# Seven products of quarters for eight in the down projections of a two-layer decoder trunk

## The chip, the cores and the metric

One core of one Trainium2 chip runs the whole program in one launch. The metric is the device time of one execution in microseconds (us). The kernel before takes 990.58 us, the median of three runs (990.31 to 990.7).

## What is computed

A two-layer trunk on x of 256 positions by 1024 features, all in float32. Cut to what matters here:

```
def swiglu(h, w_gate, w_up, w_down):
    return (silu(h @ w_gate) * (h @ w_up)) @ w_down      # 1024 -> 2816 -> 1024

for layer in (0, 1):
    h = h + 0.5 * swiglu(rmsnorm(h), ffn1_w_gate, ffn1_w_up, ffn1_w_down)
    h = h + mixer(rmsnorm(h))      # layer 0: dilated windows, layer 1: blocks
    h = h + 0.5 * swiglu(rmsnorm(h), ffn2_w_gate, ffn2_w_up, ffn2_w_down)
return rmsnorm(h)
```

So there are four SwiGLU stages, named f10 and f20 (layer 0) and f11 and f21 (layer 1), and each ends in a product of activations 256 x 2816 with down weights 2816 x 1024. These four products are the subject.

## The kernel before, in words

**Every float32 product is three products.** `parts_of` (L84) and `pieces_of` (L143) split an operand into a rounded high part, written by ScalarE (ACT) as a copy (L154 for weights), and the rest, written by VectorE (DVE) as a subtraction (L155). `product` (L180) then issues high by high (L183), high by low (L185) and low by high (L187), all into one PSUM accumulator. The tiles of weights are called wh and wl. Each name has its pool of 8 buffers, and a buffer holds 128 x 1024; raw weights have 4 buffers of 1 MB, filled by SyncE's (SP) DMA queue.

**A SwiGLU stage** is `ffn_blocks` and then `down`. `ffn_blocks` goes over 22 blocks f of 128 hidden features, two at a time: gate and up products (L194 128x512, L197 128x256, weights stationary), then ACT and DVE join, scale and multiply them (L391 to L410), and `parts_of` leaves block f as the tile act_f, features on partitions and the 256 positions side by side, high and low.

**The down product** (L359) takes its weights in 11 units u of two blocks of rows, k = 2u and 2u+1, each row block 128 x 1024. Outputs are four accumulators of 128 positions by 512 columns, (t, c) with t the half of the positions and c the half of the columns; in the program's words they are dn_f_d with t, c and an offset. For the first 18 blocks k, PE goes through all four outputs for each k: 12 matmuls of 128x512, which is 24 for a unit. The weights of the last four k are held, and each output in turn gets its last 12 matmuls, is added to h by DVE (L385, a scalar_tensor_tensor with the norm's factor), and `done` starts the next norm on it. In f10, f20 and f11 the turn is (0,0), (1,0), (0,1), (1,1), the list TURNED. In f21, the last stage, output (1,1) is two accumulators of 256 columns all the way, so that the last piece before the end is small.

**PSUM** has five banks in the pool accp (accumulators) and three in trp (transposes, and the norm's small products). `down` uses four of accp in three stages and five in f21.

**The order** on each engine is set by the framework's scheduler out of the program order, buffers and dependences; each engine runs its own queue in order. Tiles of the pool xp (one buffer for each name) hold the normed input x of a stage, one tile for each k; ap holds 22 tiles of activations; pp holds softmax tiles in the attention stages.

Of the kernel before, what the change touches and what calls it, by code (L numbers as in the profile page):

```python
# [62 lines left out]
def trunk(ctx: ExitStack, tc: tile.TileContext, a: dict, out: bass.AP):  # L63
# [291 lines left out]


    TURNED = [(0, 0, 0, 512), (1, 0, 0, 512), (0, 1, 0, 512), (1, 1, 0, 512)]

    def down(name, w, blocks, scale, segs, done, tail=4):  # L359


        accs = [acc(f"dn_{name}_{t}_{c}_{o}")[:, :n] for t, c, o, n in segs]
# [18 lines left out]
        for i, (t, c, o, n) in enumerate(segs):
            for k, ws in held:
                product(accs[i:i + 1], *lhs(k, t), [cols(i, ws)], False, k == KF - 1)
            hc = h[:, t, c * 512 + o:c * 512 + o + n]
            nc.vector.scalar_tensor_tensor(hc, accs[i], scale[t], hc, op0=ALU.mult, op1=ALU.add)  # L385
            done(*segs[i])
# [377 lines left out]
```

## Time and profile before

| | |
|---|---|
| median of three runs | 990.58 us (990.31 to 990.7) |
| the profiled execution | 990.6 us, of which its span is 988.8 us |
| PE busy in the span | 977.8 us, 99% |
| DVE busy | 692.7 us, 70% |
| ACT busy | 590.8 us, 60% |
| granted TensorE clock, mean | 0.999 |
| weights read by SP's queue | 175.55 MB, 54.9% of the 16 engines' span |

How to read it: the profile is of one execution. Its span runs from the first instruction to the last on the core, and the device time is 1.8 us longer. "Busy" counts a matmul from its start to its modelled end, and matmuls overlap, so that the mean of one (378 ns) is longer than the distance to the next; the distances between starts say what a matmul costs. "Idle before" is time in which the engine had nothing to run just before an instruction, with what ended it. A stage's limit is read from the windows and from the waits inside that stage.

### The profile page before, as it was taken

The page shows a single profiled execution, that of the slowest core. Times are in us where ns is not written, and L with a number is a line of the kernel's source. Part 1 is how long each engine was busy: PE and PEld are TensorE (multiplying, and loading weights), DVE is VectorE, ACT ScalarE, POOL GpSimd, SP SyncE. Part 2 cuts the span into 40 slices and gives each one's busy share as a digit, 9 for nine tenths or more (in the row PEclk, how much of TensorE's full clock was granted, in tenths as well). Part 3 has the DMA queues.
Part 4 walks back from the last instruction along what each step waited for, and adds up shares of the span by engine and source line. Part 5 has one row for each costly group of instructions (what it writes and reads, how often), then busy time and mean ns, then how long its engine had stood idle before and what let it go on. Part 6 is the DMA issues. An engine that isn't in the chain of part 4 may idle for free.

```text
span 988.8 us, 14084 instructions
## 1 busy us (share of the span) xinstructions
PE 977.8 (99%) x5297; PEld 832.1 (84%) x5297; DVE 692.7 (70%) x1248; ACT 590.8 (60%) x1068; POOL 58.9 (6%) x72
## 2 busy tenths in 40 slices
PE   9999999999999999999999999999999999999997
PEld 6888888888888888888888888888877888888886
DVE  7977764577786777774488777646677868777642
ACT  6766553567776656653476566436677756655531
POOL 3000000022400000000000000000142000000000
PEclk9999999999999999999999999999999999999999
DMA  9985565464344566665555665655534346555611
GB/s 319 288 261 172 175 234 188 138 206 168 128 129 132 166 194 195 207 204 181 169 171 178 206 200 183 213 192 172 190 129 149 124 148 186 182 174 199 224 43 42
DMA packets 127236, 177.00 MB, mean 179 GB/s; under 512 B 3520, under 2 KB 106176, under 8 KB 127168
## 3 DMA queue, kind: packets, MB, share of 16 engines
q1 hardware_dynamic: 126736, 175.55, 54.9%
q8 instruction: 41, 0.67, 0.3%
q10 hardware_dynamic: 432, 0.55, 0.2%
q14 instruction: 27, 0.22, 0.1%
HBM read 175.04 MB, written 1.05 MB: 178 GB/s over the span
## 4 chain that ended last, share of the span: by engine, by line
PE 93%; ACT 3%; DVE 2%; DMA 1%; issue 0%; SPq 0%; POOLq 0%; POOL 0%; ACTq 0%; DVEq 0%
PE f_g L194 16%; PE f_u L194 16%; PE f_u L197 8%; PE f_g L197 8%; PE dn_f_d L183 8%; PE dn_f_d L185 8%; PE dn_f_d L187 8%; PE qk_a L183 1%; PE qk_a L187 1%; PE qk_a L185 1%; PE x_n L275 1%; DVE wl_ao L348 1%; PE kv_b L183 1%; PE ot_ao L183 1%; PE q_b L183 1%; PE ot_ao L187 1%
## 5 line engine op out<-in xcount | busy, mean ns | idle before, releaser
L194 PE MATMUL f_g<-x_n,wh_f_g 128*128 128x512 f32 x688 | 180.2, 393 | 0.0
L194 PE MATMUL f_u<-x_n,wh_f_u 128*128 128x512 f32 x688 | 178.0, 390 | 0.0
L155 DVE TENSOR_TENSOR wl_f_d<-raw_f_d,wh_f_d 128x1024 fp32r<-128x1024 f32 x88 | 107.1, 1224 | 85.9 <-ACT wh_f_d L154 75.0
L194 PEld LDWEIGHTS f_u<-x_n,wh_f_u 128*128 128x128 f32 x688 | 129.0, 188 | 26.7
L194 PEld LDWEIGHTS f_g<-x_n,wh_f_g 128*128 128x128 f32 x688 | 123.9, 189 | 23.0 <-DVE x_n L92 0.4
L154 ACT ACTIVATE wh_f_d<-raw_f_d 128x1024 fp32r<-128x1024 f32 x88 | 91.4, 1056 | 85.3 <-PE dn_f_d L187 84.8
L155 DVE TENSOR_TENSOR wl_f_g<-raw_f_g,wh_f_g 128x1024 fp32r<-128x1024 f32 x86 | 102.7, 1221 | 43.9 <-PE f_g L197 31.6
L183 PE MATMUL dn_f_d<-wh_f_d,act_f 128*128 128x512 f32 (+1 forms) x374 | 115.3, 378 | 0.0
L185 PE MATMUL dn_f_d<-wl_f_d,act_f 128*128 128x512 f32 (+1 forms) x374 | 115.2, 378 | 0.0
L187 PE MATMUL dn_f_d<-wh_f_d,act_f 128*128 128x512 f32 (+1 forms) x374 | 114.9, 378 | 0.0
L155 DVE TENSOR_TENSOR wl_f_u<-raw_f_u,wh_f_u 128x1024 fp32r<-128x1024 f32 x86 | 104.8, 1220 | 8.1 <-ACT wh_f_u L154 8.0
L197 PE MATMUL f_u<-x_n,wl_f_u 128*128 128x256 f32 x688 | 103.2, 283 | 0.0
L197 PE MATMUL f_g<-x_n,wl_f_g 128*128 128x256 f32 x688 | 103.1, 283 | 0.0
L197 PEld LDWEIGHTS f_g<-x_n,wl_f_g 128*128 128x128 f32 x688 | 96.3, 190 | 6.6
L154 ACT ACTIVATE wh_f_g<-raw_f_g 128x1024 fp32r<-128x1024 f32 x86 | 90.3, 1054 | 12.8 <-PE f_g L194 4.0
L197 PEld LDWEIGHTS f_u<-x_n,wl_f_u 128*128 128x128 f32 x688 | 91.7, 192 | 0.1
L154 ACT ACTIVATE wh_f_u<-raw_f_u 128x1024 fp32r<-128x1024 f32 x86 | 87.4, 1050 | 7.2 <-PE dn_f_d L187 3.3
L187 PEld LDWEIGHTS dn_f_d<-wh_f_d,act_f 128*128 128x128 f32 x374 | 69.0, 188 | 13.1
L185 PEld LDWEIGHTS dn_f_d<-wl_f_d,act_f 128*128 128x128 f32 x374 | 69.0, 188 | 13.0
L183 PEld LDWEIGHTS dn_f_d<-wh_f_d,act_f 128*128 128x128 f32 x374 | 68.8, 188 | 13.0 <-DVE j_f_g L392 0.6
L408 ACT ACTIVATE j_f_g<-j_f_g 128x256 f32<-128x256 f32 x88 | 36.0, 416 | 59.3 <-DVE j_f_g L407 57.8
L90 DVE TENSOR_TENSOR act_f<-j_f_g,act_f 128x256 fp32r<-128x256 f32 x88 | 37.0, 423 | 33.7 <-ACT act_f L94 33.7
(208 smaller groups left out, 1446.2 us busy)
## 6 DMA issues: line engine op xcount, KB each, us to landing
raw_f_d<-in_ffn_w_down_dram SPq DMA_DIRECT2D x44, 1024.0 KB, 4.9
raw_f_g<-in_ffn_w_gate_dram SPq DMA_DIRECT2D x43, 1024.0 KB, 5.3
raw_f_u<-in_ffn_w_up_dram SPq DMA_DIRECT2D x43, 1024.0 KB, 5.3
raw_qka<-in_a_w_qkv_dram SPq DMA_DIRECT2D x16, 512.0 KB, 4.2
raw_va<-in_a_w_qkv_dram SPq DMA_DIRECT2D x4, 1024.0 KB, 5.1
raw_ao<-in_a_w_o_dram SPq DMA_DIRECT2D x4, 1024.0 KB, 4.9
raw_kvb<-in_kv_w_dram SPq DMA_DIRECT2D x8, 512.0 KB, 4.0
raw_qb<-in_b_w_q_dram SPq DMA_DIRECT2D x4, 1024.0 KB, 5.0
```

The source lines that it names most:

```text
L90: nc.vector.tensor_sub(lo, src, hi.bitcast(F32))
L154: nc.scalar.activation(wh, r, AF.Copy)
L155: nc.vector.tensor_sub(wl, r, wh.bitcast(F32))
L183: nc.tensor.matmul(ac, xh, wh, start=first, stop=False)
L185: nc.tensor.matmul(ac, xh, wl, start=False, stop=False)
L187: nc.tensor.matmul(ac, xl, wh, start=False, stop=last)
L194: nc.tensor.matmul(ac, wh, flat(x), start=first and i == 0, stop=False)
L197: nc.tensor.matmul(ac[:, :S], wl, x[:, 0, :], start=False, stop=last and i == len(ws) - 1)
L275: nc.tensor.transpose(tr[:, (2 * i + t) * P:(2 * i + t + 1) * P], h[:, t, k * P:(k + 1) * P], ident)
L348: self.rest.append(lambda wl=wl, raw=raw, wh=wh: nc.vector.tensor_sub(wl, raw, wh.bitcast(F32)))
L408: nc.scalar.activation(g, g, AF.Silu)
```

## The change

In each down product four of the eleven units, u in SEVEN = (1, 3, 5, 7), are multiplied by Winograd's form of Strassen's scheme. Such a unit is a 2 x 2 product of quarters: activations a11, a21 (block k = 2u, the halves of the positions), a12, a22 (block 2u+1), weights b11, b12 (block 2u, the halves of the columns), b21, b22 (block 2u+1). Eight products of quarters (24 matmuls of 128x512) become seven (21), of four sums of activations and four sums of weights.

- `add_up` (in `ffn_blocks`) forms the four sums s1 to s4 of a unit's activations when its second block is done: four DVE operations of 128x128, then `parts_of` of 128x512 (one ACT, one DVE).
- `sevenths` forms the sums of the weights, t1 with t3 in one DVE subtraction of 128x1024, t2 and t4 in one of 128x512 each, and splits b11 (128x512) and b21 with b22, t1 with t3, t2 with t4 (128x1024 each): four wh and four wl buffers for a unit where it was two of each. Its temporaries take the xp tiles x0 to x3; for that `gain` now lays two k of x into one tile.
- Three products of a unit add straight into the outputs (0,0), (0,1), (1,0) with the other units; p1, p5 and p7 gather in the three banks of trp and p6 in the fifth of accp over the four units.
- After u = 7 `gather` adds p1, p5, p6 and p7 to h: one ACT copy and two DVE additions (u, v), and six scalar_tensor_tensor, all 128x512.
- In f21 output (1,1) is one accumulator of 512 columns up to k = 17, closed after u = 8; only the held four k go into two halves of 256, in trp banks.

The diff's core:

```
+SEVEN = (1, 3, 5, 7)
...
+    def sevenths(name, j, raw):
+        both = [xp.tile([P, 2, 512], F32, tag=f"x{2 * (j % 2) + i}", name=f"t_{name}_{i}") for i in range(2)]
+        (t1, t3), (t2, t4) = [(b[:, 0], b[:, 1]) for b in both]
+        nc.vector.tensor_sub(both[0], raw[:, :, 512:], raw[:, 0, :].rearrange("p (c n) -> p c n", n=512))
+        (b11,), one = split(f"{name}_a", raw[:, 0, :512], 512)
+        one()
+        (b21, b22), two = split(f"{name}_b", raw[:, 1, :], 1024)
+        two()
+        nc.vector.tensor_sub(t2, raw[:, 1, 512:], t1)
+        nc.vector.tensor_sub(t4, raw[:, 1, :512], t2)
+        (w1, w3), three = split(f"{name}_c", flat(both[0]), 1024)
+        three()
+        (w2, w4), four = split(f"{name}_d", flat(both[1]), 1024)
+        four()
+        return b11, b21, b22, w1, w3, w2, w4
...
+        def gather():
+            close(0, 0, p1)
+            u, v = [atile([P, 512], name=f"u_{name}_{i}") for i in range(2)]
+            nc.scalar.activation(u, p1, AF.Copy)
+            nc.vector.tensor_add(u, p6, u)
+            close(0, 1, u)
+            close(0, 1, p5)
+            nc.vector.tensor_add(v, p7, u)
+            close(1, 0, v)
+            close(1, 1, v)
+            close(1, 1, p5)
...
+                for ac, x, b, mine in ((p1, a11, b11, True), (accs[0, 0], a12, b21, False), (accs[0, 1], s4, b22, False),
+                                       (p5, s1, w1, True), (p7, s3, w3, True), (p6, s2, w2, True), (accs[1, 0], a22, w4, False)):
+                    product([ac], *x, [b], first and mine, last and mine)
...
+        def add_up(u, g0, g1):
+            s = pp.tile([P, 4, P], F32, tag="pT", name=f"s_{name}_{u}")
+            a11, a21, a12, a22 = [g[:, t * P:(t + 1) * P] for g in (g0, g1) for t in range(NT)]
+            nc.vector.tensor_add(s[:, 0], a21, a22)
+            nc.vector.tensor_sub(s[:, 1], s[:, 0], a11)
+            nc.vector.tensor_sub(s[:, 2], a11, a21)
+            nc.vector.tensor_sub(s[:, 3], a12, s[:, 1])
...
-         [(0, 0, 0, 512), (0, 1, 0, 512), (1, 0, 0, 512), (1, 1, 0, 256), (1, 1, 256, 256)], finish_part)
+    down("f21_d", a["ffn2_w_down"][1], blocks, sums, n6.half, STRAIGHT, finish_part, halved=True)
```

Over the program the order has 340 rows of each of L184, L186 and L188 for the down products (332 of 128x512 and 8 of 128x256) where L183, L185 and L187 had 374 (330 and 44). DVE has 193 more instructions, ACT 52; POOL and SP have as many as before.

PE, the second half of unit 1 in f10, of the change (a, b, c, d are the four splits of the unit's weights, sums_f10_1 its sums of activations):

```order
L184 MATMUL dn_f10_d_0_1_1469<-wh_f10_d_1_b_1518,sums_f10_1_484 128x512
L186 MATMUL dn_f10_d_0_1_1469<-wl_f10_d_1_b_1519,sums_f10_1_484 128x512
L188 MATMUL dn_f10_d_0_1_1469<-wh_f10_d_1_b_1518,sums_f10_1_484 128x512
L184 MATMUL dn_f10_d_p5_1472<-wh_f10_d_1_c_1524,sums_f10_1_484 128x512 [waits Activation_49]
L186 MATMUL dn_f10_d_p5_1472<-wl_f10_d_1_c_1525,sums_f10_1_484 128x512 [waits DVE_49]
L188 MATMUL dn_f10_d_p5_1472<-wh_f10_d_1_c_1524,sums_f10_1_484 128x512
L184 MATMUL dn_f10_d_p7_1473<-wh_f10_d_1_c_1524,sums_f10_1_484 128x512
L186 MATMUL dn_f10_d_p7_1473<-wl_f10_d_1_c_1525,sums_f10_1_484 128x512
L188 MATMUL dn_f10_d_p7_1473<-wh_f10_d_1_c_1524,sums_f10_1_484 128x512
L184 MATMUL dn_f10_d_p6_1474<-wh_f10_d_1_d_1528,sums_f10_1_484 128x512 [waits PE_49,Activation_49]
L186 MATMUL dn_f10_d_p6_1474<-wl_f10_d_1_d_1529,sums_f10_1_484 128x512 [waits DVE_49]
L188 MATMUL dn_f10_d_p6_1474<-wh_f10_d_1_d_1528,sums_f10_1_484 128x512
```

Three matmuls in a row now go into one bank, and PE waits for the splits c and d separately, after 9 and 15 matmuls of the unit's 21.

DVE, the splits of the weights in f10's down product. Before, units 5 to 7:

```order
L155 TENSOR_TENSOR wl_f10_d_5_0_1616<-raw_f10_d_5_1613,wh_f10_d_5_0_1615 128x1024
L155 TENSOR_TENSOR wl_f10_d_5_1_1620<-raw_f10_d_5_1613,wh_f10_d_5_1_1619 128x1024
L155 TENSOR_TENSOR wl_f10_d_6_0_1650<-raw_f10_d_6_1647,wh_f10_d_6_0_1649 128x1024
L155 TENSOR_TENSOR wl_f10_d_6_1_1654<-raw_f10_d_6_1647,wh_f10_d_6_1_1653 128x1024
L155 TENSOR_TENSOR wl_f10_d_7_0_1684<-raw_f10_d_7_1681,wh_f10_d_7_0_1683 128x1024
L155 TENSOR_TENSOR wl_f10_d_7_1_1688<-raw_f10_d_7_1681,wh_f10_d_7_1_1687 128x1024
```

Of the change, from the last split of unit 1 to the last of unit 3:

```order
L379 TENSOR_TENSOR t_f10_d_3_0_1589<-raw_f10_d_3_1587 128x1024
L371 TENSOR_TENSOR wl_f10_d_1_d_1529<-t_f10_d_1_1_1512,wh_f10_d_1_d_1528 128x1024
L156 TENSOR_TENSOR wl_f10_d_2_0_1556<-raw_f10_d_2_1553,wh_f10_d_2_0_1555 128x1024
L156 TENSOR_TENSOR wl_f10_d_2_1_1560<-raw_f10_d_2_1553,wh_f10_d_2_1_1559 128x1024
L371 TENSOR_TENSOR wl_f10_d_3_a_1593<-raw_f10_d_3_1587,wh_f10_d_3_a_1592 128x512
L371 TENSOR_TENSOR wl_f10_d_3_b_1597<-raw_f10_d_3_1587,wh_f10_d_3_b_1596 128x1024
L384 TENSOR_TENSOR t_f10_d_3_1_1590<-raw_f10_d_3_1587,t_f10_d_3_0_1589 128x512
L371 TENSOR_TENSOR wl_f10_d_3_c_1603<-t_f10_d_3_0_1589,wh_f10_d_3_c_1602 128x1024
L385 TENSOR_TENSOR t_f10_d_3_1_1590<-raw_f10_d_3_1587,t_f10_d_3_1_1590 128x512
L379 TENSOR_TENSOR t_f10_d_5_0_1667<-raw_f10_d_5_1665 128x1024
L371 TENSOR_TENSOR wl_f10_d_3_d_1607<-t_f10_d_3_1_1590,wh_f10_d_3_d_1606 128x1024
```

A unit of seven products has seven DVE operations where a unit of eight has two, and its first subtraction stands ahead of the last split of the unit of seven before it.

DVE, the end of f10's splits, of the change (dn_f10_d_p1, p5, p6, p7 are the gathered products, wl_qka the splits of the next stage):

```order
L408 SCALAR_TENSOR_TENSOR h_85<-dn_f10_d_p1_1471,half_n0_277,h_85 128x512
L156 TENSOR_TENSOR wl_f10_d_9_1_1839<-raw_f10_d_9_1832,wh_f10_d_9_1_1838 128x1024
L156 TENSOR_TENSOR wl_f10_d_10_0_1845<-raw_f10_d_10_1842,wh_f10_d_10_0_1844 128x1024
L156 TENSOR_TENSOR wl_f10_d_10_1_1849<-raw_f10_d_10_1842,wh_f10_d_10_1_1848 128x1024
L414 TENSOR_TENSOR u_f10_d_0_1788<-dn_f10_d_p6_1474,u_f10_d_0_1788 128x512
L353 TENSOR_TENSOR wl_qka0_0_0_1946<-raw_qka0_0_1937,wh_qka0_0_0_1945 128x1024
L408 SCALAR_TENSOR_TENSOR h_85<-u_f10_d_0_1788,half_n0_277,h_85 128x512
L417 TENSOR_TENSOR u_f10_d_1_1789<-dn_f10_d_p7_1473,u_f10_d_0_1788 128x512
L408 SCALAR_TENSOR_TENSOR h_85<-dn_f10_d_p5_1472,half_n0_277,h_85 128x512
L408 SCALAR_TENSOR_TENSOR h_85<-u_f10_d_1_1789,half_n0_277,h_85 128x512
L408 SCALAR_TENSOR_TENSOR h_85<-u_f10_d_1_1789,half_n0_277,h_85 128x512
```

Before, four splits wl_qka followed on the last split of unit 10 with nothing between them; now the additions stand behind and between these splits.

## Rows read from the trace of the kernel before

**Rows 1.** The page: busy us (share of the span) of each engine, and the span in 40 slices of 24.7 us, in tenths.

```profile
PE 977.8 (99%) x5297; PEld 832.1 (84%) x5297; DVE 692.7 (70%) x1248; ACT 590.8 (60%) x1068; POOL 58.9 (6%) x72
DVE  7977764577786777774488777646677868777642
POOL 3000000022400000000000000000142000000000
PEclk9999999999999999999999999999999999999999
```

**Rows 2.** The page: shares of the chain of work that ended last.

```profile
PE 93%; ACT 3%; DVE 2%; DMA 1%; issue 0%; SPq 0%; POOLq 0%; POOL 0%; ACTq 0%; DVEq 0%
```

**Rows 3.** Busy time by window: start and end, its length, then PE, PEld, DVE, ACT, POOL busy (instructions), granted clock, DMA share, GB/s. The first three are the down products of f10, f11 and f21, then f10's gate and up products, then three us at the start of f10's down product.

```profile
132.00:193.00 61.00, 61.00 (x274) 50.18 (x273) 31.09 (x33) 26.61 (x35) 0.00 (x0) 1.00 0.57 190
619.00:680.00 61.00, 61.00 (x274) 50.20 (x273) 31.09 (x33) 26.62 (x35) 0.00 (x0) 1.00 0.56 190
921.00:983.00 62.00, 61.39 (x332) 52.64 (x330) 28.20 (x33) 19.45 (x28) 1.19 (x3) 1.00 0.28 94
20.00:132.00 112.00, 112.00 (x646) 98.96 (x646) 90.78 (x155) 74.36 (x132) 1.62 (x1) 1.00 0.72 231
134.00:137.00 3.00, 3.00 (x15) 2.47 (x14) 3.00 (x5) 2.58 (x4) 0.00 (x0) 1.00 0.88 335
```

**Rows 4.** Timeline of PE in f10's down product: start us, us of the merged piece, what. The first is the product's first matmul; 139.89, 142.61 and 145.33 are one k step (12 matmuls of 128x512) apart; from 180.69 to 188.17 there are 33 matmuls in turn into single accumulators; L275 are transposes of the next norm.

```profile
131.66 0.63 PE L183 MATMUL dn_f_d<-wh_f_d,act_f 128*128 128x512 f32 x2
139.89 0.61 PE L183 MATMUL dn_f_d<-wh_f_d,act_f 128*128 128x512 f32 x2
142.61 0.61 PE L183 MATMUL dn_f_d<-wh_f_d,act_f 128*128 128x512 f32 x2
180.69 0.39 PE L183 MATMUL dn_f_d<-wh_f_d,act_f 128*128 128x512 f32 x1
188.17 0.39 PE L183 MATMUL dn_f_d<-wh_f_d,act_f 128*128 128x512 f32 x1
188.86 0.60 PE L275 MATMUL x_n<-ident,h 128*128 128x128 f32 x4
```

**Rows 5.** Timeline of PE in f21's down product: its first matmul; one k step, 962.82 to 965.62, of which the first 1.40 us are six matmuls of 128x512 and the rest three of 128x512 and six of 128x256; 971.19 is the first of the last four k; 982.11 the last matmul.

```profile
920.99 0.63 PE L183 MATMUL dn_f_d<-wh_f_d,act_f 128*128 128x512 f32 x2
962.82 0.64 PE L183 MATMUL dn_f_d<-wh_f_d,act_f 128*128 128x512 f32 x2
964.22 0.63 PE L183 MATMUL dn_f_d<-wh_f_d,act_f 128*128 128x512 f32 x3
965.62 0.62 PE L183 MATMUL dn_f_d<-wh_f_d,act_f 128*128 128x512 f32 x2
971.19 0.40 PE L183 MATMUL dn_f_d<-wh_f_d,act_f 128*128 128x512 f32 x1
982.11 0.28 PE L187 MATMUL dn_f_d<-wh_f_d,act_f 128*128 128x256 f32 x1
```

**Rows 6.** Waits within 132 to 190 us: who waited for whom, us in total, times, the longest.

```profile
ACT wh_f_d L154 <- PE dn_f_d L187: 20.3, 13, 1.7
DVE wl_f_d L155 <- ACT wh_f_d L154: 18.5, 13, 1.5
```

**Rows 7.** Timeline of DVE and of ACT at the start of f10's down product: two splits in a row, then the two operations behind them; and a load of ACT's function table.

```profile
130.42 2.36 DVE L155 TENSOR_TENSOR wl_f_d<-raw_f_d,wh_f_d 128x1024 fp32r<-128x1024 f32 x2 [1.28 <-PE f_g L197]
132.70 0.42 DVE L392 TENSOR_TENSOR j_f_g<-f_g,j_f_g 128x256 f32<-128x256 f32 x1
133.03 0.42 DVE L392 TENSOR_TENSOR j_f_u<-f_u,j_f_u 128x256 f32<-128x256 f32 x1
136.01 1.28 ACT L124 ACT_TABLE_LOAD   x1
```

**Rows 8.** Groups of instructions by line and form, whole span: count | busy us, mean ns of one | idle before, and what ended it. The last is from the opening, where POOL works too.

```profile
L155 DVE TENSOR_TENSOR wl_f_d<-raw_f_d,wh_f_d 128x1024 fp32r<-128x1024 f32 x88 | 107.1, 1224 | 85.9 <-ACT wh_f_d L154 75.0 <-PE f_g L197 10.9
L154 ACT ACTIVATE wh_f_d<-raw_f_d 128x1024 fp32r<-128x1024 f32 x88 | 91.4, 1056 | 85.3 <-PE dn_f_d L187 84.8
L90 DVE TENSOR_TENSOR qkl_a<-qt_a,qkh_a 128x512 fp32r<-128x512 f32 x8 | 5.5, 690 | 2.4 <-ACT qkh_a L94 2.4
L171 ACT ACTIVATE wh_u<-raw_u 128x512 fp32r<-128x512 f32 x4 | 2.5, 614 | 0.0
L385 DVE SCALAR_TENSOR_TENSOR h<-dn_f_d,half_n,h 128x512 f32<-128x512 f32 x15 | 11.2, 749 | 25.8 <-PE dn_f_d L187 25.8
L496 DVE TENSOR_TENSOR ra_a<-rt_a,rot 128x128 f32<-128x128 f32 x8 | 2.7, 342 | 2.2 <-ACT rt_a L623 2.2
L172 DVE TENSOR_TENSOR wl_u<-raw_u,wh_u 128x512 fp32r<-128x512 f32 x4 | 3.8, 954 | 0.1
```

**Rows 9.** Timeline in f10's early gate and up products: DVE's splits of the up weights for f = 6 and 7, and PE's first use of them.

```profile
40.71 2.35 DVE L155 TENSOR_TENSOR wl_f_u<-raw_f_u,wh_f_u 128x1024 fp32r<-128x1024 f32 x2
47.20 1.12 PE L197 MATMUL f_u<-x_n,wl_f_u 128*128 128x256 f32 x8
```

**Rows 10.** DMA issues: KB of one, median us from issue to landing.

```profile
raw_f_d<-in_ffn_w_down_dram SPq DMA_DIRECT2D x44, 1024.0 KB, 4.9
```

More of the change, by code (lines that the diff above doesn't have):

```diff
@@ L197, in products_t @@
                 nc.tensor.matmul(ac[:, :S], wl, x[:, 0, :], start=False, stop=last and i == len(ws) - 1)
+    pairs = {}
     def gain(k, gi, name, src, tag="x"):
-        x = xp.tile([P, 2, S], F32R, tag=f"{tag}{k}", name=f"x_{name}_{k}")
+        if k % 2 == 0:
+            pairs[tag] = xp.tile([P, 2, 2, S], F32R, tag=f"{tag}{k // 2}", name=f"x_{name}_{k}")
+        x = pairs[tag][:, k % 2]
         g = gT[:, gi * KD + k:gi * KD + k + 1]
@@ L357, in trunk, with split, rest @@
     TURNED = [(0, 0, 0, 512), (1, 0, 0, 512), (0, 1, 0, 512), (1, 1, 0, 512)]
-    def down(name, w, blocks, scale, segs, done, tail=4):
-        accs = [acc(f"dn_{name}_{t}_{c}_{o}")[:, :n] for t, c, o, n in segs]
+    STRAIGHT = [(0, 0, 0, 512), (0, 1, 0, 512), (1, 0, 0, 512), (1, 1, 0, 512)]
+    def split(name, src, n):
+        wh, wl = [wp.tile([P, n], F32R, tag=tag, name=f"{tag}_{name}") for tag in ("wh", "wl")]
+        nc.scalar.activation(wh, src, AF.Copy)
+        def rest():
+            nc.vector.tensor_sub(wl, src, wh.bitcast(F32))
+        return [(wh[:, i:i + 512], wl[:, i:i + 512]) for i in range(0, n, 512)], rest
@@ L376, in down @@
                     for t in range(NT):
-                        mine = [i for i, seg in enumerate(segs) if seg[0] == t]
-                        product([accs[i] for i in mine], *lhs(k, t), [cols(i, ws) for i in mine], k == 0, False)
+                        ends = halved and t == 1 and k == KF - tail - 1
+                        for cs in ([0], [1]) if ends else ([0, 1],):
+                            product([accs[t, c] for c in cs], *lhs(k, t), [cols(ws, c) for c in cs], k == 0, ends and cs == [1])
                 else:
                     held.append((k, ws))
[L381 to L386, printed above, removed]
+        if halved:
+            close(1, 1, accs[1, 1])
+        for t, c, _, _ in segs:
+            split_ = halved and (t, c) == (1, 1)
+            for o, n in ((0, 256), (256, 256)) if split_ else ((0, 512),):
+                ac = trt(f"dn_{name}_{t}_{c}_{o}")[:, :n] if split_ else accs[t, c]
+                for k, ws in held:
+                    product([ac], *lhs(k, t), [cols(ws, c, o, n)], split_ and k == KF - tail, k == KF - 1)
+                close(t, c, ac, o)
+                done(t, c, o, n)
     def joined(ac, name):
@@ L413, in close @@
             blocks.append(x)
-        done = []
+            gs.append(g)
+            if f % 2 and f // 2 in SEVEN:
+                add_up(f // 2, *gs[-2:])
+        def add_up(u, g0, g1):
[5 more added lines that the diff above has]
+            nc.vector.tensor_sub(s[:, 3], a12, s[:, 1])
+            x = ap_.tile([P, 2, 4, P], F32R, tag=f"qk{'hl'[len(sums) % 2]}", name=f"sums_{name}_{u}", bufs=2)
+            parts_of(x[:, 0], x[:, 1], s)
+            sums.append(x)
+        done, gs, sums = [], [], []
         def close_all():
@@ L452, in ffn_blocks @@
         close_all()
-        return blocks
+        return blocks, sums
     def ffn(name, layer, which, norm, after, first=None, beside=()):
         wg, wu, wd = (a[f"ffn{which}_w_{n}"][layer] for n in ("gate", "up", "down"))
-        blocks = ffn_blocks(name, wg, wu, norm, first, beside)
+        blocks, sums = ffn_blocks(name, wg, wu, norm, first, beside)
         if which == 1:
             table(AF.Exp, blocks[-1][:, 0, 0:1].bitcast(F32))
-        down(f"{name}_d", wd, blocks, norm.half, TURNED, lambda t, c, o, n: after.done(t, c))
+        down(f"{name}_d", wd, blocks, sums, norm.half, TURNED, lambda t, c, o, n: after.done(t, c))
     def out_x(name, pieces, base, blocks, norm, tail=3):
@@ L705, in trunk @@
         nc.sync.dma_start(gfin[c], a["final_norm"].rearrange("(o d) -> o d", o=1)[:, c * 512:(c + 1) * 512].to_broadcast([P, 512]))
-    blocks = ffn_blocks("f21", a["ffn2_w_gate"][1], a["ffn2_w_up"][1], n6)
+    blocks, sums = ffn_blocks("f21", a["ffn2_w_gate"][1], a["ffn2_w_up"][1], n6)
     parts = [[], []]
```

24 lines of the change are left out of this document (20 added, 4 removed).

## The prediction, made before the changed kernel ran

> **What bounds the kernel now.** I read the page first, then the chain, the windows of the four down products, and PE's timeline inside them. PE is busy for 977.8 of 988.8 us, at a granted clock of nine tenths or more in every slice, which is the 2.4 GHz level [rows 1], and 93% of the chain that ended last is PE's [rows 2]. In the down products PE is never idle, while DVE works 31.09 of 61.00 us and ACT 26.6 [rows 3]. The waits there all lie on the other engines: ACT waits for PE to free a buffer of weights, DVE waits for ACT [rows 6]. So a matmul taken out of a down product shortens the program by its distance to the next, as long as DVE and ACT keep ahead.
>
> That distance is 0.2267 us for 128x512: a k step of 12 takes 142.61 − 139.89 = 2.72 us, and 33 matmuls in a row into single banks take 188.17 − 180.69 = 7.48 us, the same [rows 4]. Three in a row into one bank, as the new products have them, therefore cost nothing more. Two stretches are slower. The first 36 matmuls of f10's down product take 8.23 us, 0.2286 each [rows 4], where DVE is busy all the time [rows 3]. And in f21, where 128x512 and 128x256 are mixed, the first 18 k take 971.19 − 920.99 = 50.20 us, 2.79 a step; even the six matmuls of 128x512 that stand together take 1.40 us, 0.2333 each [rows 5].
>
> **Part 1, seven for eight.** A unit loses 3 matmuls, 0.68 us; four units a stage, 2.72 us; in f10, f20 and f11 together 8.16 us off PE. Nothing else moves on PE's queue: its rows outside the down products read as before.
>
> **Part 2, f21's accumulator of 512.** Up to k = 17 the 256-column pairs become matmuls of 512 columns. I price them as in the other stages, since the instructions are then the same: 10 k at 2.72 and 4 units of 21 × 0.2267 = 4.76 us make 46.24 us for the 50.20, a gain of 3.96 us, of which 2.72 is the seven for eight. If f21's matmuls stay at 0.2333, the 204 take 47.6 us and the gain is 2.6.
>
> Together 12.1 us.
>
> **Part 3, DVE.** This is what could take it back. Lone durations: 1.224 us for 128x1024, 0.690 for 128x512 [rows 8]. One behind the other they cost less: two splits and the start of the next take 132.70 − 130.42 = 2.28 us, 1.14 each, and 128x256, 0.42 us long, comes every 0.33 [rows 7]; so about 0.09 overlaps, and 128x512 should come every 0.60 (estimate from these rows). A unit of seven has four operations of 1024 and three of 512: 4 × 1.14 + 3 × 0.60 = 6.4 us, or 7.0 at lone durations; a unit of eight 2.3 or 2.45. A pair of units costs DVE 8.6 to 9.4 us, and PE 45 × 0.2267 = 10.2. ACT has 0.614 + 3 × 1.056 = 3.8 and 2.1 us [rows 8], 5.9 a pair. So DVE goes from about half busy to 85–92% busy and stays second.
>
> The Trainium skill, "VectorE: DVE Perf Modes", section "The DRAIN you can't avoid", says that the next DVE operation does not start until the pipe of the one before is empty, which read strictly gives the 9.4; the 1.14 against 1.224 says that starts do overlap the recorded ends a little. The time would be the same by both, the margin 0.8 us a pair by the page and 1.6 by the row.
>
> Is the lead there at the start? Let T be the start of the down product. The first subtraction of unit 1 waits for PE's last read of x, since its temporaries lie on x's tiles, so it starts about T. Up to the last split of unit 1 stand, in DVE's queue, four operations of 1024, two of 512 and five of 256 of the last gate and up block: 4 × 1.14 + 2 × 0.60 + 5 × 0.33 = 7.4 us. PE needs that split at 5.44 + 16 × 0.2267 = 9.07 us. Lead 1.7 us, the smallest of the stage; ACT's load of the table, 1.28 us [rows 7], falls into it and is covered. Three pairs later the last split of unit 7 is done at T + 33.3 (35.6 at lone durations), needed at T + 39.7. The lead grows. Buffers: a unit of seven takes four of the eight pairs, the next unit two, so the queue is never more than a unit and a half ahead; raw weights land 4.9 us after issue [rows 10] and their issues come over ten us ahead.
>
> **Part 4, `gather`.** One ACT copy and eight DVE operations of 128x512, 0.69 to 0.75 us each [rows 8], about 5.8 us, start when unit 7 ends, T + 40.8, among the last splits. DVE has nothing else but five or six splits until the first output closes at T + 49. I put its end at T + 48.4. The next reader is the norm's transposes, at 188.86 − 131.66 = T + 57.2 before [rows 4] and 2.7 earlier now, which need the three banks and h: 6 us in hand. Cost nothing; without that cover 1 to 2 us a stage.
>
> **Part 5, `add_up`.** Four operations of 128x128 (0.342 from PSUM, an upper bound) and one of 512: 1.7 to 2.1 us of DVE, 0.61 of ACT, four times a stage, among gate and up products where DVE has 90.78 of 112 us at worst [rows 3]. The tightest place is f10's start: the splits of f = 6 end at 43.06 and PE uses them from 47.20 [rows 9], a lead of 4.1; it falls to about 2. Nothing.
>
> **Part 6, a busier DVE.** The start of the down products shows 0.0019 us more for each matmul under a full DVE. After the change DVE is nearly full for 180 matmuls a stage: 0.35 us, less what is in it already, 1.1 us in all four. The bounds are 0 (no link) and 0.0066 a matmul (f21's rate).
>
> **The sum.** 990.6 us of the profiled execution, which is the median (990.58) to 0.02, − 12.1 + 1.1 = **979.6 us**.
>
> **The rivals.**
>
> *A slower beat of matmuls.* All 204 matmuls up to unit 8 go at f21's 0.2333 in every stage: 204 × 0.0066 = 1.35 us lost in three stages, and f21 gains 2.6 for 3.96. The gain is 12.1 − 5.4 = 6.7: 983.9 us. For it: that rate exists and its cause is not shown. Against: it is seen only where widths are mixed, and with DVE nearly idle.
>
> *DVE loses part of its lead.* In units of seven, splits c and d wait in turn for ACT, which waits for DVE's sums. With lone durations and 0.3 us lost at each of five waits a pair costs 10.9 us against 10.2; over four pairs 2.8 us, less the lead of 1.7, about 1.1 us a stage, some 4 us: 984. For it: the chain of sums and copies is new; against: DVE has the next units' work to fill waits.
>
> *DVE becomes the bound, and the kernel slower.* DVE's operations with two inputs in SBUF run at the opening's rate, 0.954 us for 128x512 instead of 0.690 [rows 8], a factor of 1.38. Then the last split of unit 7 is done at T + 46 and PE stands 6.3 us in each stage against 2.7 won: 990.6 + 4 × 3.6 = 1005 us. It decides from a factor of 1.27 on (33.3 × 1.27 = 39.7 + 2.7). Against: those operations stand in the opening, where POOL works [rows 1], and POOL has 0.00 us in the down products of f10 and f11 [rows 3]. The Trainium skill, "SBUF — State Buffer", section "Who interferes with whom", puts such a loss down to GpSimd reading through DVE's second port; by that the rival needs POOL and falls away here.
>
> *No change.* DVE's factor lies near 1.27, or half of the down products stall: within 2 us of 990.6. That the work isn't removed is excluded: the order has 340 rows for 374 of each of the three lines.
>
> **How the numbers follow.** The forecast has 0.66 (977.5 to 982), the slower beat 0.11, part of the lead lost 0.13, no change 0.04, slower 0.06. The first three are all faster by over 0.2% (2 us, about what a measurement of this kernel can tell from no change): 0.90. The range goes from 977.5, which is the sum without part 6 and one us of luck in the tail, up to 985.5, which takes in both rivals with a remainder of f10's tight start; that leaves out some 0.15.
>
> **What would show it.** Right: PE busy without idle in the down products; unit 1 of seven takes 4.76 us from p1 to the next unit; f10's down product from its first matmul to the first transpose 54.5 to 54.9 us instead of 57.2; f21 up to the held k in 46.3 to 47; DVE 50 to 55 of 58 us in those windows, its waits for ACT short. Wrong: idle time of PE before L186 or L188 of p5 or p6 put down to DVE (lead lost); matmul distances of 0.23 and more with no idle (beat); a 128x512 subtraction well above 0.69 us (slower); PE waiting before L275 for DVE's additions (gather).

## The result, and the profile after

The changed kernel takes 978.47 us (median of four runs, 978.26 to 978.84) where the kernel before, run beside it, takes 990.64 (990.31 to 990.95): a ratio of 0.9878, with a 95% interval of 0.9861 to 0.9895. The prediction was 979.6 us, in a range of 977.5 to 985.5.

The page after: busy us and shares (the span is 976.4 us), DVE in 40 slices, and the chain.

```profile
PE 965.0 (99%) x5195; PEld 820.6 (84%) x5195; DVE 795.8 (82%) x1441; ACT 619.7 (63%) x1120; POOL 59.3 (6%) x72
DVE  7987889877786788879888887997677868778895
PE 93%; DVE 3%; ACT 3%; DMA 1%; issue 0%; POOLq 0%; POOL 0%; ACTq 0%; DVEq 0%
```

PE lost 12.8 us of work and kept its share of the span and of the chain; DVE gained 103 us and ACT 29, nearly all beside PE. Against [rows 1, 2] this is the picture of a kernel still bound by the same engine.

Windows over the down products of f10, f20, f11 and f21, with columns as in [rows 3]:

```profile
131.00:192.00 61.00, 61.00 (x276) 50.43 (x276) 55.37 (x65) 38.67 (x51) 0.00 (x0) 1.00 0.61 207
430.00:490.00 60.00, 60.00 (x274) 49.66 (x272) 54.55 (x65) 36.41 (x50) 0.00 (x0) 1.00 0.66 211
612.00:672.00 60.00, 60.00 (x273) 49.61 (x272) 54.19 (x64) 37.64 (x50) 0.00 (x0) 1.00 0.62 211
912.00:971.00 59.00, 58.00 (x270) 48.42 (x269) 51.94 (x63) 30.00 (x42) 1.19 (x3) 1.00 0.33 116
```

DVE is at about 90% in these stages where it was at half, and PE is still busy all the time (f21's last matmul ends 1 us before its window does). PE's list of waits shows it too: none of its eight entries is in a down product, and these are its longest four:

```profile
PE busy L114 <- DVE fill L111: 1.4, 1, 1.4
PE s_b L601 <- DVE pT_b L91: 0.9, 1, 0.9
PE pt_b L627 <- DVE nm_b L609: 0.8, 1, 0.8
PE f_g L198 <- DVE wl_g L173: 0.4, 2, 0.2
```

PE's timeline in f10, to be read against [rows 4]: the first matmul (T = 131.55; T is the start of a stage's down product), the start of unit 1 (p1), of unit 2, of unit 3, and the first transpose.

```profile
131.55 0.63 PE L184 MATMUL dn_f_d<-wh_f_d,act_f 128*128 128x512 f32 x2
137.02 0.39 PE L184 MATMUL dn_f_d_p<-wh_f_d_a,act_f 128*128 128x512 f32 x1
141.78 0.62 PE L184 MATMUL dn_f_d<-wh_f_d,act_f 128*128 128x512 f32 x2
147.22 0.39 PE L184 MATMUL dn_f_d_p<-wh_f_d_a,act_f 128*128 128x512 f32 x1
185.98 0.60 PE L280 MATMUL x_n<-ident,h 128*128 128x128 f32 x4
```

A unit of seven takes 141.78 − 137.02 = 4.76 us, the next unit of eight 5.44, to the hundredth what was worked out, and the first transpose comes at T + 54.43 instead of T + 57.20. In f21 ([rows 5] before) the first 18 k take 958.81 − 912.54 = 46.27 us instead of 50.20:

```profile
912.54 0.63 PE L184 MATMUL dn_f_d<-wh_f_d,act_f 128*128 128x512 f32 x2
958.81 0.39 PE L184 MATMUL dn_f_d<-wh_f_d,act_f 128*128 128x512 f32 x1
```

The two profiled spans differ by 12.4 us (the median times by 12.2). From the starts of the four down products in both traces they fall to the stages like this. The last column is the prediction's parts 1 and 2, without the 1.1 us of part 6:

| stretch | before | after | less | parts 1 and 2 |
|---|---|---|---|---|
| start to f10's T | 131.66 | 131.55 | 0.11 | 0 |
| f10's T to f20's T | 301.59 | 298.85 | 2.74 | 2.72 |
| f20's T to f11's T | 185.19 | 182.33 | 2.86 | 2.72 |
| f11's T to f21's T | 302.55 | 299.81 | 2.74 | 2.72 |
| f21's T to the end | 67.81 | 63.86 | 3.95 | 3.96 |

DVE's timeline in f10: unit 1's last split (the second row) between its neighbours, the stall and last split of unit 7, the last of `gather`'s additions; and, of PE, the second matmul of p6 in unit 1 and in unit 7, which need those splits.

```profile
136.18 1.22 DVE L379 TENSOR_TENSOR t_f_d<-raw_f_d 128x1024 f32<-128x1024 f32 x1
137.32 1.22 DVE L371 TENSOR_TENSOR wl_f_d_d<-t_f_d,wh_f_d_d 128x1024 fp32r<-128x1024 f32 x1
138.46 2.35 DVE L156 TENSOR_TENSOR wl_f_d<-raw_f_d,wh_f_d 128x1024 fp32r<-128x1024 f32 x2
163.65 1.23 DVE L371 TENSOR_TENSOR wl_f_d_d<-t_f_d,wh_f_d_d 128x1024 fp32r<-128x1024 f32 x1 [1.21 <-ACT wh_f_d_d L368]
178.68 0.75 DVE L408 SCALAR_TENSOR_TENSOR h<-dn_f_d_p,half_n,h 128x512 f32<-128x512 f32 x1
140.65 0.39 PE L186 MATMUL dn_f_d_p<-wl_f_d_d,sums_f 128*128 128x512 f32 x1
171.25 0.39 PE L186 MATMUL dn_f_d_p<-wl_f_d_d,sums_f 128*128 128x512 f32 x1
```

Unit 1's last split ends at T + 7.0 (7.4 forecast), 2.1 us ahead of PE; unit 7's at T + 33.3 (33.3 forecast), 6.4 us ahead; `gather` at T + 47.9 (48.4 forecast). The stall of 1.21 us for ACT is one of the waits of the second rival. It exists, and the lead covers it.

The prices that had only bounds, by form:

```profile
L379 DVE TENSOR_TENSOR t_f_d<-raw_f_d 128x1024 f32<-128x1024 f32 x16 | 19.5, 1219 | 10.3 <-PE f_u L198 10.3
L384 DVE TENSOR_TENSOR t_f_d<-raw_f_d,t_f_d 128x512 f32<-128x512 f32 x16 | 10.9, 684 | 0.0
L408 DVE SCALAR_TENSOR_TENSOR h<-u_f_d,half_n,h 128x512 f32<-128x512 f32 x12 | 8.6, 744 | 0.0
L491 DVE TENSOR_TENSOR s_f<-j_f_g,j_f_g 128x128 f32<-128x128 f32 x16 | 4.5, 283 | 0.0
```

All lie where the nearest rows of before put them, or below. The first row's idle time is DVE waiting for PE's last read of x, 2.6 us a stage, since the temporaries lie on x's tiles.

### The profile page after: what moved, and what is told of

It is laid out like the page before. It is cut to its first block, busy times and chain, and to the rows that moved or that the text cites. A ratio compares the mean times of both kernels' runs of the same rounds, so it can differ in the third digit from the quotient of the medians.

```text
span 976.4 us, 14147 instructions
## 1 busy us (share of the span) xinstructions
PE 965.0 (99%) x5195; PEld 820.6 (84%) x5195; DVE 795.8 (82%) x1441; ACT 619.7 (63%) x1120; POOL 59.3 (6%) x72
## 4 chain that ended last, share of the span: by engine, by line
PE 93%; DVE 3%; ACT 3%; DMA 1%; issue 0%; POOLq 0%; POOL 0%; ACTq 0%; DVEq 0%
PE f_g L195 16%; PE f_u L195 16%; PE f_u L198 9%; PE f_g L198 8%; PE dn_f_d L188 6%; PE dn_f_d L186 6%; PE dn_f_d L184 6%; PE dn_f_d_p L188 1%; PE dn_f_d_p L186 1%; PE dn_f_d_p L184 1%; PE qk_a L184 1%; PE qk_a L188 1%; PE qk_a L186 1%; PE x_n L280 1%; DVE wl_ao L353 1%; PE kv_b L184 1%
## 5 line engine op out<-in xcount | busy, mean ns | idle before, releaser
L184 PE MATMUL dn_f_d<-wh_f_d,act_f 128*128 128x512 f32 (+1 forms) x228 | 75.4, 387 | 0.0
L188 PE MATMUL dn_f_d<-wh_f_d,act_f 128*128 128x512 f32 (+1 forms) x228 | 75.4, 387 | 0.0
L186 PE MATMUL dn_f_d<-wl_f_d,act_f 128*128 128x512 f32 (+1 forms) x228 | 75.3, 387 | 0.0
L156 DVE TENSOR_TENSOR wl_f_d<-raw_f_d,wh_f_d 128x1024 fp32r<-128x1024 f32 x56 | 65.9, 1218 | 5.5 <-PE f_g L198 5.5
L460 ACT ACTIVATE j_f_g<-f_g 128x256 f32<-128x256 f32 x88 | 33.1, 376 | 52.7 <-PE f_g L198 51.9
L95 ACT ACTIVATE act_f<-j_f_g 128x256 fp32r<-128x256 f32 x88 | 36.0, 411 | 41.3 <-DVE j_f_g L479 41.3
L155 ACT ACTIVATE wh_f_d<-raw_f_d 128x1024 fp32r<-128x1024 f32 x56 | 56.4, 1048 | 6.0 <-PE dn_f_d L188 5.7
L460 ACT ACTIVATE j_f_u<-f_u 128x256 f32<-128x256 f32 x88 | 33.5, 380 | 33.2 <-PE f_u L198 23.6
```

Source lines behind the costliest of these rows:

```text
L95: nc.scalar.activation(hi, src, AF.Copy, scale=scale)
L155: nc.scalar.activation(wh, r, AF.Copy)
L156: nc.vector.tensor_sub(wl, r, wh.bitcast(F32))
L460: nc.scalar.activation(s, ac[:, S:], AF.Copy)
```

## The experiments

The theory: PE's sum of matmul distances is the time, as long as DVE's last split of unit 7 comes before T + 39.7. Rivals: f21's slow matmuls belong to the last stage and not to the mixed widths; DVE is so nearly full that the gain hangs on its last per cents; or DVE's load does not matter at all.

**e1_eight: all units by eight, f21's accumulator wide.**

```
-SEVEN = (1, 3, 5, 7)
+SEVEN = ()
```

> All 22 blocks by eight products again; of the change only the one accumulator of 512 columns in f21 (and x's tiles in pairs) stays. Theory (time is PE's sum of distances, mixed widths cost 0.0066 us a matmul): f21's first 18 k take 18 x 2.72 = 48.96 us instead of 50.20, 1.2 us off the kernel before, 989.4 us; the other three down products as before, 61.0 us each. Rival (f21's matmuls are slow because it is the last stage, with idle DVE): f21 stays at 2.79 a step, 990.6 us.

Measured: 989.37 us (989.22 to 989.77), ratio 0.9988 (0.9978 to 0.9998). f21's first 18 k:

```profile
920.92 0.63 PE L184 MATMUL dn_f_d<-wh_f_d,act_f 128*128 128x512 f32 x2
969.95 0.39 PE L184 MATMUL dn_f_d<-wh_f_d,act_f 128*128 128x512 f32 x1
```

969.95 − 920.92 = 49.03 us, 2.724 a step, with DVE as idle as before. So the 0.2333 belonged to the mixing of widths, not to the stage, and the stretch from f21's T to the end is 1.2 us shorter. The rest, 989.37 − 978.47 = 10.9 us, is what seven for eight brings in four stages: 4 × 2.72.

**e2_load1, e3_load3, e5_load4, e6_load6: more work for DVE.** An unused subtraction, n times in each unit of seven (n = 1, 3, 4, 6):

```
         two()
+        spare = xp.tile([P, D], F32, tag="spare", name=f"spare_{name}")
+        for _ in range(n):
+            nc.vector.tensor_sub(spare, raw[:, 1, :], raw[:, 0, :])
```

> The changed kernel with one more DVE subtraction of 128x1024 (1.14 us, its result unused) in each unit of seven. Theory (DVE ends its last split of unit 7 6.4 us before PE needs it): the lead falls by about 3 us, PE waits for nothing, 978.5 us. Rival (DVE is nearly the bound, the gain hangs on its last per cents): 1 to 3 us lost a stage, 982 to 990.

> The changed kernel with three more DVE subtractions of 128x1024 in each unit of seven. Theory: the last split of unit 7 moves from T + 33.3 to T + 41.5 to 44, PE needs it at T + 39.7: 2 to 4.5 us of PE waits a stage, and more where the additions after unit 7 reach the transposes; 988 to 997 us, which is the point where DVE takes back what seven products win (a factor of about 1.3 on DVE). Rival (PE is held by something else, DVE has room): under 982.

> The changed kernel with four more DVE subtractions of 128x1024 in each unit of seven; by the order nine of the sixteen of a stage now stand between T and the last split of unit 7 (the others fall into idle time ahead of T). Theory (PE waits only where DVE's last split comes later than T + 39.7): 33.3 - 1.2 of idle + 9 x 1.14 = T + 42.4, 2.7 us of PE waits in each of four stages, 10.8 in all, and up to 1.5 more at the start of each of three next stages: 989 to 994 us, the time before the change. Rival (DVE's lead hardly matters, PE is held by the norms alone): 981 to 984.

> As the run with four, with six more DVE subtractions a unit of seven, some sixteen of 24 after T. Theory: the last split of unit 7 at T + 33.3 - 1.2 + 16 x 1.14 = T + 50.3, a factor of 1.5 on DVE, 10.6 us of PE waits a stage, 42 in all, and some at the next stages: 1020 to 1026 us, slower than before the change. Rival (lead hardly matters): under 990.

Measured:

| n | time (us) | last split of unit 7 in f10 | T to first transpose in f10 |
|---|---|---|---|
| 0 | 978.47 | T + 33.3 | 54.43 |
| 1 | 978.13 | T + 35.3 | 54.43 |
| 3 | 980.19 | T + 38.5 | 54.44 |
| 4 | 990.30 | T + 42.4 | 57.29 |
| 6 | 1034.92 | T + 49.2 | 68.38 |

The threshold was put at T + 39.7, and it lies between T + 38.5 (n = 3, no wait) and T + 42.4 (n = 4, waits). With n = 1 the lead falls by 2.0 us, not 3, since only two of the four extra subtractions stand between T and that split; PE waits for nothing there. With n = 3 my expectation of 988 to 997 was wrong, and by its input, not by the rule: DVE's timeline shows that of the twelve extra subtractions only six stand after T (from 146.00 to 166.65), the others ahead of it in DVE's idle time, and that they fill the stall of 1.21 us. The split should then come at 33.3 − 1.2 + 6 × 1.14 = T + 38.9, and it came at T + 38.5, ahead of T + 39.7. PE waited nowhere in the down products; 1.4 us of span were lost elsewhere, 1.14 of it between f20's T and f11's (183.47 for 182.33). That loss lies just behind f20's down product, at the turn to the next stage, where PE has two waits that the kernel after hasn't:

```profile
490.68 0.50 PE L195 MATMUL f_u<-x_n,wh_f_u 128*128 128x512 f32 x1 [0.29 <-ACT wh_f_u L155]
491.56 0.50 PE L195 MATMUL f_g<-x_n,wh_f_g 128*128 128x512 f32 x1 [0.38 <-DVE x_n L93]
```

Before the run with n = 4 I counted them from the order: nine after T, split at T + 42.4, and it ended at T + 42.4 (172.75 + 1.25 − 131.64):

```profile
171.62 1.24 DVE L386 TENSOR_TENSOR spare_f_d<-raw_f_d 128x1024 f32<-128x1024 f32 x1
172.75 1.25 DVE L371 TENSOR_TENSOR wl_f_d_d<-t_f_d,wh_f_d_d 128x1024 fp32r<-128x1024 f32 x1
```

PE's longest waits in its down products are ones that were missing in the kernel after, 4, 4 and 3 of them, at most one of each in a stage:

```profile
PE dn_f_d_p L186 <- DVE wl_f_d_d L371: 2.2, 4, 0.6
PE dn_f_d_p L184 <- ACT wh_f_d_d L368: 1.3, 4, 0.3
PE dn_f_d L186 <- DVE wl_f_d L156: 1.1, 3, 0.4
```

A stage loses 57.29 − 54.43 = 2.86 us (2.7 forecast), and the gain is gone: 0.9996 (0.9986 to 1.0006) of the time before. That is the threshold of the third rival made to happen: the time to unit 7's last split has grown by a factor of 42.4 / 33.3 = 1.27. With n = 6 it is slower by 4.5% (ratio 1.0446, 1.0425 to 1.0467), 9 us beyond its expectation. A stage loses 14 us where the split alone says 10.6 at most. Two of the extra operations also stand ahead of unit 8's splits, so that f10's longest wait comes there. And the granted clock falls behind some of the waits, from the 2.4 GHz level to 1.2 for part of a window: to 0.85 where PE had waited 1.55 us, to 0.72 behind 2.67 us. It did not fall behind the longest wait, 3.00 us. The windows of 5 us (columns as in [rows 3]) and the two longest waits:

```profile
160.00:165.00 5.00, 3.23 (x11) 1.98 (x9) 5.00 (x6) 4.22 (x5) 0.00 (x0) 0.85 0.01 3
175.00:180.00 5.00, 2.68 (x6) 1.94 (x7) 5.00 (x6) 3.79 (x4) 0.00 (x0) 0.72 0.11 43
185.00:190.00 5.00, 3.28 (x13) 2.44 (x14) 5.00 (x8) 1.15 (x2) 0.00 (x0) 1.00 0.60 201
177.32 0.79 PE L184 MATMUL dn_f_d_p<-wh_f_d_d,sums_f 128*128 128x512 f32 x1 [2.67 <-ACT wh_f_d_d L368]
185.35 0.50 PE L186 MATMUL dn_f_d<-wl_f_d,act_f 128*128 128x512 f32 x1 [3.00 <-DVE wl_f_d L156]
```

**e7_pool: POOL does a part.**

```
-        nc.vector.tensor_sub(both[0], raw[:, :, 512:], ...
+        (nc.gpsimd if j else nc.vector).tensor_sub(both[0], raw[:, :, 512:], ...
```

> The changed kernel with the first subtraction of the units 3, 5 and 7 (128x1024, two inputs in SBUF) on POOL. Theory A (two-input DVE operations get slower while POOL reads SBUF, as in the opening, 0.954 for 0.690 us): DVE's splits that run beside POOL lengthen by up to 1.38, those without it stay at 1.22 and 0.69; 3.4 us of DVE work a stage is gone, PE still waits for nothing, 978.5 us. Theory B (the 0.954 of the opening has another cause): no DVE operation in the down products lengthens, 978.5 us as well.

Measured: 978.51 us, ratio 0.9877 (0.9857 to 0.9897), no wait of PE in the down products, so both theories had the time right. Of the mechanism each had only half. POOL's subtraction for unit 5, DVE's split of 128x512 (of unit 3) beside it, and the next such split (of unit 5) without POOL:

```profile
141.62 3.32 POOL L379 TENSOR_TENSOR t_f_d<-raw_f_d 128x1024 f32<-128x1024 f32 x1 [6.98 <-DVE wl_f_d L156]
142.58 2.91 DVE L371 TENSOR_TENSOR wl_f_d_a<-raw_f_d,wh_f_d_a 128x512 fp32r<-128x512 f32 x1
151.09 0.68 DVE L371 TENSOR_TENSOR wl_f_d_a<-raw_f_d,wh_f_d_a 128x512 fp32r<-128x512 f32 x1
```

One DVE operation takes 2.91 us instead of 0.68 and ends 0.55 us after POOL's; the others around it keep 0.69 and 1.22. Nothing is slowed by a factor: one operation is held until POOL's is nearly over. Of the twelve subtractions on POOL eight have such a DVE operation beside them (1.97 us for 0.42, 2.91 for 0.68 or 3.43 for 1.22) and take 2.91 to 3.32 us themselves. Beside the other four none is held, and there POOL takes 5.57 to 6.19, DVE running on without a break for the first 3.3 to 3.9 us and then waiting some 2.3 us for POOL. The opening of the kernel before fits this once its four are taken apart (min, median, max in ns): two take 0.68 to 0.69 us, two 1.22, where I had read a factor from their mean of 954:

```profile
L172 DVE TENSOR_TENSOR wl_u<-raw_u,wh_u x4: 681/955/1223, 6.8 to 16.3; 128x512 fp32r<-128x512 f32 x4
```

**e4_five: a fifth unit of seven, u = 8, in all stages** (its sums in a tile of their own; in f21 output (1,1) closes after u = 6).

```
-SEVEN = (1, 3, 5, 7)
+SEVEN = (1, 3, 5, 7, 8)
```

> The changed kernel with a fifth unit of seven products, u = 8, in every stage. Theory: 3 matmuls of 0.2267 less in each of four stages, 2.7 us off: 975.8 us; DVE has 4.1 us more a stage, its last split of unit 8 at about T + 39 to 40, needed at T + 44.4, and the additions end near T + 52, needed by T + 53.7. Rival (DVE is full): the additions reach the transposes and the gain is lost, 978 to 982.

**e8_five_pool: the same with POOL's subtractions.**

> Five units of seven (u = 8 added) with the first subtraction of the units 3, 5, 7 and 8 on POOL: 4.6 us less DVE work a stage than the run with five. Theory (the fifth unit's gain was given back because DVE came late to the next norm): DVE is as free as in the changed kernel, the down products keep their 0.8 us each and the next stages start as early: 975.5 to 976.2 us. Rival (POOL slows DVE's operations by 1.38 while it reads): no gain over the run with five, 977.2 to 979.

**e9_five_last: the fifth unit in f21 alone; e10_five_own: in f10, f20 and f21, unit 1's temporaries in f10 and f20 on tiles of their own.** The edit for the temporaries:

```
+        own = j == 0 and name[:3] in ("f10", "f20")
-        both = [xp.tile([P, 2, 512], F32, tag=f"x{2 * (j % 2) + i}", ...
+        both = [xp.tile([P, 2, 512], F32, tag=f"kx{i}" if own else f"x{2 * (j % 2) + i}", ...
```

> The changed kernel with the fifth unit of seven (u = 8) in f21 alone, the stage behind which no norm and no weights' splits of a next stage follow. Theory (in the other three stages the fifth unit's 0.68 us was given back at the next stage's start): f21 keeps its 0.68 us, the rest is as in the changed kernel: 977.8 us, as much as five units in all four. Rival (the loss is in the down products or in gate and up): no more than a quarter of the run with five's gain, 978.3.

> Five units of seven in f10, f20 and f21, four in f11; in f10 and f20 the temporaries of unit 1 lie on tiles of their own (kx0, kx1) and no longer wait for PE's last read of x, so that three DVE operations (1.14 + 2 x 0.60 us) move ahead of T, where DVE idles for 2.57 us. Theory (it is DVE's late start on the next stage that gave the gain back): DVE's queue is 2.3 us less behind after f10 and f20, these stages keep most of their 0.68 us: 976.4 to 977 us. Rival (the queue's length does not matter, the norm's chain itself is later): as the run before, 977.7.

Measured: e4_five 977.72 us (977.23 to 978.14; ratio 0.9868, 0.9853 to 0.9884), e9_five_last 977.70 (0.9872, 0.9856 to 0.9889), e10_five_own 977.30 (977.11 to 977.35; 0.9866, 0.9852 to 0.9881), e8_five_pool 988.50 (0.9978, 0.9969 to 0.9988).

By stretches, as above, from one profile of each. e9_five_last and the changed kernel multiply by the same units up to f21 and differ by up to 0.07 us there, so a tenth of a us says little:

| stretch | after | e4_five | e9_five_last | e10_five_own |
|---|---|---|---|---|
| start to f10's T | 131.55 | 131.81 | 131.59 | 131.56 |
| f10's T to f20's T | 298.85 | 299.06 | 298.78 | 298.72 |
| f20's T to f11's T | 182.33 | 181.90 | 182.33 | 181.92 |
| f11's T to f21's T | 299.81 | 299.61 | 299.81 | 299.78 |
| f21's T to the end | 63.86 | 63.32 | 63.39 | 63.32 |

Each fifth unit should leave 3 × 0.2267 = 0.68 us. The additions of `gather` end in time, as expected, and PE waits in no down product. But in e4_five f21 keeps 0.54 of it, f20 0.43 and f11 0.20, and f10's stretch is 0.21 longer, though f10's down product itself is 0.84 us shorter from its first to its last matmul (57.18 for 58.02). PE's timeline shows the main place, a transpose of the next norm that waits for DVE:

```profile
194.71 0.39 PE L186 MATMUL qk_a<-wl_qka,x_n 128*128 128x512 f32 x1
195.51 0.44 PE L280 MATMUL x_n<-ident,h 128*128 128x128 f32 x2 [0.42 <-DVE x_n L93]
```

DVE ahead of it. In e4_five's order two splits of the next stage and half_n, which here waits for POOL, stand between v_n and this x_n; in the kernel after there is one split, and half_n comes behind x_n. The end of that piece:

```profile
193.77 0.17 DVE L251 TENSOR_SCALAR half_n<-c_n 128x2 f32<-128x2 f32 x1 [0.59 <-POOL c_n L249]
193.85 1.22 DVE L353 TENSOR_TENSOR wl_va<-raw_va,wh_va 128x1024 fp32r<-128x1024 f32 x1
194.98 0.87 DVE L93 SCALAR_TENSOR_TENSOR x_n<-x_n,gT,x_n 128x256 fp32r<-128x256 f32 x2
```

So most of the fifth unit's gain is given back, in f10, at DVE's turn from one stage to the next: at T + 70 PE is only 0.16 us ahead of the changed kernel. f11 has the same wait, 0.44 us, and 0.17 left at T + 70. The other 0.37 us that f10's stretch loses come later, and were not followed up. e9_five_last has its time as expected, but its reason only in part: e4_five wins 0.63 us in f20's and f11's stretches and loses 0.47 ahead of T and in f10's; the 0.26 ahead of T lie in the opening, where the fifth unit has no work and the runs differ anyway (131.46 to 131.81). e10_five_own was to bring f10 back, and f10's transposes have the same wait, 0.42 us at 195.31, with 0.13 us kept; in f20 it keeps 0.41, as e4_five does without the remedy. The remedy gave at most 0.34 us, and its range (976.4 to 977.0) was missed by 0.3. It brought unit 1's last split to T + 1.1 from T + 7.0, but DVE then waits for ACT, and the last split of unit 8 ends at T + 38.7 where it was T + 38.6 in e4_five. The two rows, e10_five_own's first:

```profile
169.00 1.22 DVE L375 TENSOR_TENSOR wl_f_d_d<-t_f_d,wh_f_d_d 128x1024 fp32r<-128x1024 f32 x1 [1.50 <-ACT wh_f_d_d L372]
169.22 1.23 DVE L371 TENSOR_TENSOR wl_f_d_d<-t_f_d,wh_f_d_d 128x1024 fp32r<-128x1024 f32 x1 [0.22 <-ACT wh_f_d_d L368]
```

So DVE's queue was no shorter at the turn, and the run can't tell its theory from its rival. Whether the order of the split and x_n costs there or the length of DVE's queue stays open: no run moved that split alone, or shortened the queue. e10_five_own is the fastest here, 1.2 us under the changed kernel, its runs clear of the other's (977.35 and 978.26 at the nearest); the two ratios' intervals overlap, so that a gain over four units is likely and not shown.

e8_five_pool missed by 12 us, and is slower than e4_five by 10.8. In f10 the last two of POOL's four subtractions (units 7 and 8) take 7.90 us together, the first took 2.97, and a DVE sum beside them takes 2.87 us:

```profile
151.89 7.90 POOL L379 TENSOR_TENSOR t_f_d<-raw_f_d 128x1024 f32<-128x1024 f32 x2 [7.03 <-DMA raw_f_d<-in_ffn_w_down_dram]
157.47 2.87 DVE L384 TENSOR_TENSOR t_f_d<-raw_f_d,t_f_d 128x512 f32<-128x512 f32 x1 [2.30 <-POOL t_f_d L379]
```

ACT's last copy for unit 7 then waits 4.73 us for its sum (to 164.46), `gather`'s last addition starts at 186.71 instead of 183.47 in e4_five, and PE's transposes wait for h. In sum these are PE's longest waits of the run:

```profile
PE x_n L280 <- DVE h L408: 5.2, 5, 1.5
```

f10's down product takes 60.20 us to its last matmul there, f20's 59.57 and f11's 60.22, for 57.18, 56.72 and 57.18 in e4_five; f21's, with no norm's transposes in it, 56.50, as in e4_five. From f21's T to the end it takes 65.5 us for 63.3 all the same: the work behind the last matmul comes later.

## Why the prediction was right, point by point

- **What bounds.** Right: PE's share of span and chain is unchanged, and its matmuls come every 0.2267 us, three in a row into one bank too.
- **Part 1.** Right: 2.74, 2.86 and 2.74 us for 2.72 in the three stages. Within each down product it is 2.77, 2.76 and 2.77, the 0.05 more being the faster start of part 6; the other 0.10 of f20's stretch lie behind its down product and were not followed up.
- **Part 2.** Right: 3.95 for 3.96. The rate of 0.2267 instead of 0.2333 was a choice between two rows; e1_eight shows it alone.
- **Part 3.** Right in size and place: leads of 2.1 and 6.4 us for 1.7 and 6.4. Pitches of 1.14 and 0.60 were the right choice against lone durations, which would have put the split at T + 35.6. That the gain is gone at a factor of 1.27 is shown by e5_load4.
- **How DVE's operations overlap, and what holds them.** Three of 128x1024 in a row start at 136.18, 137.32 and 138.46, so the measured 1.14 us decides. The Trainium skill, "VectorE: DVE Perf Modes", section "The DRAIN you can't avoid", says that the next operation does not start until the pipe is empty, which read strictly gives 1.22 for each. The same section of the Trainium skill adds that a next operation that is not held starts earlier, and with that the trace agrees. In e7_pool a two-input subtraction beside POOL takes 2.91 for 0.68 us. The Trainium skill, "SBUF — State Buffer", section "Who interferes with whom", says of two-port operations that the one that issues first gets the port pair for its whole instruction and the other fully blocks, and of two-input operations that they contend; e7_pool shows the block for a two-input one. The prediction's reading, that this needs POOL, kept the slower rival's chance low, and rightly: POOL did 0.00 us in the windows of f10, f20 and f11, and 1.19 in f21's.
- **Part 4 and part 5.** Right: nothing. PE waits for neither `gather` nor `add_up`. The 0.342 us that part 5 took as read from PSUM is a row whose inputs, rt_a and rot, are SBUF tiles; `add_up`'s operations take 0.283.
- **Part 6.** Wrong, and it is the 1.1 us by which the forecast is too high: without it the sum is 978.5. It took the slower first 36 matmuls of f10 (0.2286) as the price of a full DVE on every matmul. After the change DVE is fuller for 50 us, and from T + 5.5 on the distance is 0.2267; the first 36 take 8.19 us (the second row below is the start of the 37th) where they took 8.23. Of the 0.07 us that they lost before, 0.04 are gone, and with them a wait: before, one load of stationary data (PEld) in each down product waited 0.16 us for DVE's L392, which stood behind two splits [rows 7] (first row below, all four stages). After the change one subtraction (131.03) stands ahead of it, L461 there (132.17), and no load waits. So DVE seems to have had a part, by one late operation and not by a rate. The other 0.03 us are there after the change as well (unit 0 takes 5.47 us instead of 5.44), always behind gate and up's matmuls of 256 columns; e1_eight's f21 loses the whole 0.07 again (49.03 for 48.96), with the wait. No run took those matmuls away, so their part in it stays open.

```profile
PEld dn_f_d L183 <- DVE j_f_g L392: 0.6, 4, 0.2
139.74 0.39 PE L184 MATMUL dn_f_d_p<-wh_f_d_c,sums_f 128*128 128x512 f32 x1
```

- **The slower rival** named the right threshold and the wrong mechanism: a factor of 1.38 on all two-input operations shows in no run; e7_pool shows single operations held.

## What to carry to other kernels

Where one engine is busy without idle and the others wait for it, the gain of leaving out its instructions is their count times the distance between starts, and the question is the lead of the second engine at its tightest place, counted in its own queue: here 2.1 us at the first unit and 6.4 at the last, with the gain gone where DVE's time to that last split is 1.27 times as long. Read from the queue's order what really lies between two points before pricing a dose (e3_load3 was wrong by that alone), and do not read a rate from a mean of few (four operations of 0.68 and 1.22 us made 0.954). Near the break the sum of the second engine's work is no longer the whole answer: the fifth unit fits by its lead, and PE still waited 0.42 us for DVE at the turn to the next stage.

## What the runs showed of the hardware that was not expected

- A DVE subtraction with two inputs in SBUF can be held as a whole beside a running POOL operation: 2.91 us for 0.68. Beside eight of e7_pool's twelve POOL operations one was held; the other four POOL operations took 5.57 to 6.19 us instead of 2.91 to 3.32, and ended some 2.3 us after DVE's queue had stopped.
- Matmuls of 512 columns next to matmuls of 256 columns come every 0.2333 us, among themselves every 0.2267 (f21 before, and e1_eight).
- Behind waits of PE of 1.55 and 2.67 us the granted clock fell to 0.85 and 0.72 in windows of 5 us, and behind one of 3.00 us it stayed at 1.00 (f10 in e6_load6); waits of up to 0.6 us in the down products left the run's mean at 0.998 (e5_load4). What decides it stays open.
